# An S5 state-space mixer on one core: the sums for a transposed matrix move from TensorE to GpSimd, and the normed input is made in three parts in three different pairs

## The chip, the cores and the metric

One core of one Trainium2 chip. The metric is the device time of one execution in microseconds (us), and the median of three runs stands for a kernel. The engines are named as in the profile: PE is TensorE, DVE VectorE, ACT ScalarE, POOL GpSimd, and SP is SyncE, whose queue issues most of the DMAs.

## The reference, cut to what matters

The reference is one inference step of a two-layer diffusion backbone for 1,024 noisy tokens and 128 context tokens with 1,024 channels. Layer 0 mixes the tokens with an S5 state-space layer in two directions, layer 1 with a Fourier transform, and a gated convolutional FFN follows each. Only the S5 mixer is touched here:

```python
def s5_direction(u, lam_re, lam_im, log_dt, b_re, b_im, c_re, c_im, h0, reverse):
    dt = jnp.exp(log_dt)[:, None]
    abar = jnp.exp(lam * dt)                      # (64 groups, 64 states), complex
    bbar = ((abar - 1.0) / lam)[..., None] * bmat  # (groups, states, 16 channels)
    bu = jnp.einsum('blgc,gpc->blgp', u, bbar)
    bu = bu.at[:, edge].add(abar * h0)
    _, h = lax.associative_scan(_linear_recurrence, (a, bu), axis=1, reverse=reverse)
    y = jnp.real(jnp.einsum('gcp,blgp->blgc', cmat, h))
    return y, h[:, edge]
# h = rms_norm(x, g_mix) * (1 + sc1) + sh1 is the input u; both directions are summed,
# a diagonal term is added, then GELU and a gated linear layer (GLU)
```

## The kernel before, in words

The schedule is written out by hand (`manual_schedule`): each engine executes its instructions in the order in which the program emits them, and semaphores come from the tiles that instructions share.

The mixer works in frames of 8 tokens. A frame's 8 tokens and a group's 16 channels are one axis of 128, and the recurrence goes from frame to frame, 128 frames for the sample and 16 for the context (146 columns with the edges). The 64 groups go in 8 batches (b = 0 to 7) of 8 groups, and a batch in 4 pairs of groups (pr = 0 to 3). One turn of the loop in `run` is one pair i = 4b + pr. It emits, in this order:

- `vmm(i+1)`: 16 products on PE with the transposed input matrix `PT` (L1503) into one of two PSUM tiles `V`
- `scan(i)` on DVE (L1544), `vin(i+1)` on DVE (L1524 to L1527, a rotation by the tables `sn` and `cs`; L1524 reads `sn`, L1525 reads `cs`), with four small ACT copies behind it, and `vout(i)` on DVE (L1555 to L1557)
- `decay(i+2)` on ACT (L1539), `wmm(i-1)`: 36 products on PE (L1567, L1573) and their eviction `ysb` on ACT (L1579)
- then two lists, `fill` and `late`, with pieces that make the matrices of the batches to come. `vin(i+1)` of pair 3 belongs to the next batch already, and reads that batch's tables.

The pieces, with who executes them:

- `make_u(b)` makes the normed input `hb`: part 0 is one product for the context (t0 = 8), parts 1 and 2 are four products each (L1475, on PE), each part in a PSUM bank of tag "misc" with an ACT eviction (L1479). `load_u(b)` sends `hb` to the tile `u` by 8 DMAs; `load_x(b)` fetches the tile `xb`, of which there is one.
- `make_ca(b)` returns pieces of the output matrix `CA`: five on GpSimd (L1365 to L1370, of which `ca[3:]` are L1369 and L1370), `ends` (four ACT copies, L1374 and L1375) and a pair `bb`. `bb[0]` (`real`) makes the real part of `Bb` (L1383 to L1385, on GpSimd for b > 2), `bb[1]` makes the imaginary part on DVE (L1383 to L1385 again), then L1392 and L1393 on DVE, both of which read the real part too, and an ACT copy (L1394).
- `make_p(b)` returns the products `P` (L1417, three of 128x512 for each half, on GpSimd for b > 1, with one small sum L1412 ahead) and the transposes `tr` (L1425): for each half two calls, each of which fills one "misc" bank and evicts it on ACT (L1428) into `PT`. Half 0 is used by pairs 0 and 1, half 1 by pairs 2 and 3.
- `make_t(b)`: 64 products on PE (L1447) in both "misc" banks, six ACT evictions (L1457 to L1459), two small sums on GpSimd (L1460, L1461) and DMAs that spread the result.
- `tables(b)`: `tb[0]` (L1308, L1309 on DVE), `tb[1]` (L983, L984 on DVE and an ACT op), `tb[2]` (`sn`) and `tb[3]` (`cs`), both on ACT (L1322).

There are two "misc" banks. A piece that takes one of them again waits until its last content has been evicted. In the kernel before the pieces lie so, for a batch b from 1 to 5: pair 0 has the products of half 0, `tb[0]`, `bb[0]`; pair 1 the products of half 1, `ca[:1]`, the transposes of half 0 and `tb[1:]`; pair 2 `bb[1]`, `ca[1:3]`, `make_t` and the transposes of half 1; pair 3 `ca[3:]`, `ends`, all three parts of `make_u` and `load_x`.

Of the kernel before, what the change touches and what calls it, by code (L numbers as in the profile page):

```python
# [13 lines left out]
OP = mybir.AluOpType  # L14
# [950 lines left out]
class Ssm:  # L965
# [431 lines left out]
    def make_p(self, b):  # L1397


        nc, sp, V = self.nc, self.sp, self.nc.vector  # L1400
        gs = slice(8 * b, 8 * b + 8)
        Bb, Bx = self.Bb[b], self.Bx[b]
        PT = self.PT[b] = [sp.tile([128, 2, 4, 128], F32, tag=f"PT{h}", bufs=1, name="PT") for h in range(2)]
        x = [t[:, :, None, :].to_broadcast([128, 8, 8, 16]) for t in (Bb[:, 0, :, 0], Bx[:, 1], Bx[:, 0])]
        qs, Ps = [], {}
        E = nc.gpsimd if b > 1 else V

        def prod(h, i):
            def f():
                if not qs:  # L1410
                    qs.append(self.sg.tile([128, 8, 8], F32, tag="gs", bufs=1, name="gs"))
                    E.tensor_tensor(qs[0], self.G[:, 0, gs], self.G[:, 1, gs], OP.add)  # L1412
                if i == 0:
                    Ps[h] = self.sg.tile([128, 3, 4, 8, 16], F32, tag="P", bufs=2, name="P")
                g = (qs[0], self.G[:, 1, gs], self.G[:, 0, gs])[i]
                hs = slice(4 * h, 4 * h + 4)
                E.tensor_tensor(Ps[h][:, i], g[:, hs, :, None].to_broadcast([128, 4, 8, 16]), x[i][:, hs], OP.mult)  # L1417
            return f

        def tr(ri, half):  # L1420
            def f():
                p = self.bank("misc", 2)
                for i in range(4):
                    for k in (0, 1 + ri):
                        nc.tensor.matmul(p[:, i * 128:(i + 1) * 128],  # L1425
                                         lhsT=Ps[half][:, k, i].rearrange("p a b -> p (a b)"),
                                         rhs=self.ident, start=k == 0, stop=k > 0, is_transpose=True)
                nc.scalar.activation(PT[half][:, ri].rearrange("p a b -> p (a b)"), p, AF.Copy)  # L1428
            return f
        return [[prod(h, i) for i in range(3)] for h in range(2)], [[tr(ri, h) for ri in range(2)] for h in range(2)]  # L1430

    def make_t(self, b):

# [31 lines left out]
            src = bass.AP(tensor=self.kd.tensor, offset=o + (7 - t) * 16, ap=[[240, 16], [32 * 240, 8], [1, 128]])  # L1465
            nc.sync.dma_start(T[16 * t:16 * t + 16], src)

    def make_u(self, b, between=None):

        nc, sp = self.nc, self.sp  # L1470
        x, h = self.xb[b] if b else [t[:, :128] for t in self.xt], self.hb
        for t0, n in ((8, 1), (4, 4), (0, 4)):
            p = self.bank("misc", 2)
            for i in range(n):
                nc.tensor.matmul(p[:, 128 * i:128 * i + 128], lhsT=x[t0 + i], rhs=self.R[:, t0 + i], start=True, stop=True)  # L1475
            if n == 1 and between:
                between()
            o, c = (h[:, t0:t0 + 4, 0:128], 0) if n > 1 else (h[:, :, 130:146], 1)
            nc.scalar.activation(o, p[:, :128 * n].rearrange("p (t k) -> p t k", t=o.shape[1]), AF.Identity,  # L1479
                                 scale=self.a1[:, b, c:c + 1], bias=self.b1[:, b, c:c + 1])  # L1480
            if n == 1:

                nc.scalar.activation(h[:, 7, 128:129], h[:, 0, 130:131], AF.Copy)
                nc.scalar.activation(h[:, 0, 129:130], h[:, 7, 145:146], AF.Copy)
# [108 lines left out]
    def run(self):  # L1593
# [16 lines left out]
        ca, ends, bb = self.make_ca(0)  # L1610
# [6 lines left out]
        pp, tr = self.make_p(0)  # L1617
        tb = self.tables(0)
# [8 lines left out]
        ca1, ends1, bb = self.make_ca(1)  # L1627
# [17 lines left out]
        tb = self.tables(1)  # L1645
# [4 lines left out]
        n = 32  # L1650
        for i in range(n + 1):
            b, pr = divmod(i, 4)
            n1, n2 = b + 1 < 8, b + 2 < 8
            if 1 < i + 1 < n:
                self.vmm(i + 1)
            if i < n:
                self.scan(i)
            if i + 1 < n:
                self.vin(i + 1)
            if i < n:  # L1660
                self.vout(i)
            if i + 2 < n:
                self.decay(i + 2)
            if i:
                self.wmm(i - 1)
            while self.m_ada:
                self.ada_end()
            if i == n:
                self.store_y(b - 1)
                self.n.want(("g", 1), self.nc.vector)  # L1670
                break
            if i == 27:
                self.made.__exit__(None, None, None)
            fill, late = [], []
            if pr == 0:
                if n1 and b:
                    self.load_u(b + 1)
                if b:
                    self.store_y(b - 1)
                if n1:  # L1680
                    pp, tr = self.make_p(b + 1)
                    fill = list(pp[0])
                    if b:
                        tb = self.tables(b + 1)
                        fill += tb[:1]
                if n2 and b:
                    ca, ends, bb = self.make_ca(b + 2)
                    fill.append(lambda: bb[0](self.nc.gpsimd))
                if not b:
                    fill += ca1[2:] + [ends1]  # L1690
                    second = Later(self.nc.vector)
                    self.phases(second, rest)
                    self.phases16(second, rest)
                    late = tr[0] + tb[2:3] + [lambda: self.powers(rest, [second])]
            if pr == 1:
                if n1:
                    fill = list(pp[1])
                    late = tr[0] + tb[1:] if b else tb[3:]
                if not b:
                    ca, ends, bb = self.make_ca(2)  # L1700
                if n2:
                    fill += ca[:1]
                    if b + 3 < 8:
                        self.loads(b + 3)
            if pr == 2:
                if n1:
                    late = [lambda: self.make_t(b + 1)()] + tr[1]
                if n2:
                    if not b:
                        bb[0]()  # L1710
                    bb[1]()
                    fill = ca[1:3]
            if i == 7:
                late = [self.last_frame]
            if pr == 3 and n2:
                fill = ca[3:] + [ends]
                late.append(lambda: self.make_u(b + 2))
                if b + 3 < 8:
                    late.append(lambda: self.load_x(b + 3))
            if i >= 27:  # L1720
                late.append(lambda: self.n.early(i - 27))
            call(fill)
            if i == n - 1:
                self.finals()
            call(late)
# [154 lines left out]
```

## Time and profile before

| | us |
|---|---|
| median of 3 runs (2441.09 to 2443.05) | 2441.32 |
| the profiled execution, whole | 2443.08 |
| its span, first to last instruction | 2441.3 |
| PE busy in the span | 2303.3 (94%) |
| DVE busy | 1487.1 (61%) |
| ACT busy | 870.0 (36%) |
| POOL busy | 679.7 (28%) |

The profiled execution lies 1.8 us above the median, and 1.8 us of its time lie outside the span. The mean of PE is that of the whole kernel: the GLU and the two FFNs after the mixer keep PE busy nearly all the time. The mixer ends near 322 us. In its loop, from 100 to 320 us, PE is busy 14.5 to 18.4 us of each 20, and DVE 13.0 to 19.7.

### The profile page before, as it was taken

Reading aid. Unit: us, or ns where it says so; the run is one execution under the profiler, and the core shown is the slowest. Engines: PE = TensorE matmul, PEld = TensorE weight load, DVE = VectorE, ACT = ScalarE, POOL = GpSimd, SP = SyncE. Lnnn points to the kernel's source line nnn. Section 1 sums busy time; section 2 is a strip of 40 time slices with the busy share of each in tenths; the row PEclk is TensorE's granted clock in tenths of the full one; section 3 lists DMA queues with packets and bytes.
Section 4 is the critical chain, followed back from the end, with each engine's and each line's share of the span. In section 5 each row is a group of like instructions: output and inputs, shape, how many; then the busy total and the mean of one; then the engine's idle time right before and its main releaser. Section 6 shows DMA issues by size and latency. Waiting matters only on the chain.

```text
span 2441.3 us, 35730 instructions
## 1 busy us (share of the span) xinstructions
PE 2303.3 (94%) x14754; PEld 2223.2 (91%) x14754; DVE 1487.1 (61%) x2407; ACT 870.0 (36%) x1320; POOL 679.7 (28%) x462
## 2 busy tenths in 40 slices
PE   3788899999999999999999999999999999999996
PEld 3677788788999999999999999899999999999996
DVE  7877869797635555455544574855554455644456
ACT  5555563225432223222232254442223222232234
POOL 6465303234211122112221253521222112221124
PEclk8899999999999999999999999999999999999998
DMA  6432297671110111111110131111111111111112
GB/s 215 123 83 72 74 300 251 225 241 35 61 44 27 44 44 52 35 35 43 44 52 26 53 105 38 44 52 35 44 44 52 35 35 35 52 52 36 28 42 78
DMA packets 94522, 182.33 MB, mean 75 GB/s; under 512 B 16948, under 2 KB 57204, under 8 KB 93336
## 3 DMA queue, kind: packets, MB, share of 16 engines
q1 hardware_dynamic: 90824, 170.67, 22.2%
q0 software_dynamic: 2096, 6.62, 0.8%
q8 instruction: 117, 1.92, 0.3%
q10 hardware_dynamic: 1440, 2.75, 0.3%
q14 instruction: 45, 0.37, 0.0%
HBM read 163.70 MB, written 11.53 MB: 72 GB/s over the span
## 4 chain that ended last, share of the span: by engine, by line
PE 69%; DVE 16%; issue 6%; POOL 3%; DMA 3%; ACT 2%; SPq 1%; DVEq 0%; ACTq 0%; POOLq 0%
PE acc L199 62%; DVE c L308 3%; DVE dl L602 2%; DVE dh L602 2%; PE f L839 2%; DMA w_ada<-w_ada 1%; DVE X L916 1%; DVE h L222 1%; PE f L749 1%; DVE X L363 1%; DVE X L364 1%; POOL P L1417 1%; PE misc L1447 1%; PE f L199 1%; PE V L1503 1%
## 5 line engine op out<-in xcount | busy, mean ns | idle before, releaser
L199 PE MATMUL acc<-h,uh 128*128 128x384 f32 (+1 forms) x4992 | 1016.0, 338 | 0.5 <-ACT ysb L1579 0.5
L199 PEld LDWEIGHTS acc<-h,uh 128*128 128x128 f32 x4992 | 885.9, 188 | 15.0 <-issue 12.0
L183 POOL TENSOR_TENSOR ul<-raw,uh 128x1024 fp32r<-128x1024 f32 x104 | 271.4, 2609 | 1243.3 <-ACT uh L182 1243.3
L199 PE MATMUL acc<-h,ul 128*128 128x384 f32 (+1 forms) x2496 | 571.7, 337 | 0.0
L308 DVE SCALAR_TENSOR_TENSOR c<-t,cw,c 128x896 f32<-128x896 f32 x704 | 347.2, 562 | 202.4 <-ACT c L305 202.4
L199 PEld LDWEIGHTS acc<-h,ul 128*128 128x128 f32 x2496 | 448.8, 189 | 0.0
L182 ACT ACTIVATE uh<-raw 128x1024 fp32r<-128x1024 f32 x108 | 113.7, 1052 | 548.0 <-PE acc L199 495.4
L300 DVE COPY wb<-acc 128x2 f32<-128x2 f32 x88 | 14.0, 159 | 406.3 <-PE acc L199 406.3
L363 DVE SCALAR_TENSOR_TENSOR X<-acc,MOD,X 128x768 f32<-128x768 f32 x168 | 169.8, 1011 | 118.3 <-PE acc L199 118.3
L199 PE MATMUL acc<-gh,dh 128*128 128x384 f32 x960 | 220.7, 337 | 18.4 <-DVE X L365 18.4
L199 PE MATMUL acc<-gl,dh 128*128 128x384 f32 x960 | 218.5, 335 | 0.0
L199 PE MATMUL acc<-gh,dl 128*128 128x384 f32 x960 | 218.3, 334 | 0.0
L199 PEld LDWEIGHTS acc<-gh,dh 128*128 128x128 f32 x960 | 168.8, 188 | 26.9 <-PE acc L199 23.6
L199 PEld LDWEIGHTS acc<-gh,dl 128*128 128x128 f32 x960 | 171.4, 188 | 0.0
L199 PEld LDWEIGHTS acc<-gl,dh 128*128 128x128 f32 x960 | 171.2, 188 | 0.0
L336 ACT ACTIVATE gh<-c 128x1152 fp32r<-128x1152 f32 x44 | 51.4, 1169 | 329.2 <-DVE c L331 290.9
L303 ACT ACTIVATE t<-t,wb 128x1024 f32<-128x1024 f32 x88 | 101.4, 1153 | 152.2 <-DVE t L301 152.2
L183 POOL TENSOR_TENSOR dl<-raw,dh 128x1024 fp32r<-128x1024 f32 x40 | 99.8, 2515 | 165.1 <-ACT dh L182 165.1
L305 ACT ACTIVATE c<-t,cb,cw 128x1152 f32<-128x1152 f32 x88 | 118.9, 1351 | 2.9
L301 DVE TENSOR_TENSOR t<-acc,R 128x1152 f32<-128x1152 f32 x88 | 118.6, 1348 | 0.0
L326 ACT ACTIVATE c<-c 128x1152 f32<-128x1152 f32 x44 | 51.4, 1167 | 152.4 <-DVE c L308 152.3
L602 DVE SCALAR_TENSOR_TENSOR dl<-w_ada,SC,dl 128x1024 f32<-128x1024 f32 x50 | 88.8, 1815 | 0.0
(327 smaller groups left out, 2600.9 us busy)
## 6 DMA issues: line engine op xcount, KB each, us to landing
raw<-w_up SPq DMA_DIRECT2D x88, 512.0 KB, 3.6
w_ada<-w_ada SPq DMA_DIRECT2D x80, 512.0 KB, 4.8
raw<-w_down SPq DMA_DIRECT2D x44, 512.0 KB, 3.6
w_ada<-w_ada SPq DMA_DIRECT2D x8, 1024.0 KB, 5.0
raw<-w_glu SPq DMA_DIRECT2D x16, 512.0 KB, 4.7
u<-hb SPq DMA_DIRECT2D x64, 73.0 KB, 2.8
y_scratch<-ysb SPq DMA_DIRECT2D x8, 584.0 KB, 3.9
xt<-x SPq DMA_DIRECT2D x9, 512.0 KB, 8.1
```

What stands on the lines that cost most here:

```text
L182: nc.scalar.activation(hi, raw, AF.Copy)
L183: (E or nc.gpsimd).tensor_tensor(lo, raw, hi.bitcast(F32), OP.subtract)
L199: mm(outs[j], lhsT=w, rhs=r[j], start=first and i == 0, stop=last and i == 2)
L301: nc.vector.tensor_tensor(t.rearrange("p (a b) -> p a b", a=3), p[:, :, :384], self.R.rearrange("p (a b) -> p a b", a=3), OP.mult)
L303: nc.scalar.activation(t[:, :NS], t[:, :NS], AF.Identity, bias=wb[:, 0:1])
L305: nc.scalar.activation(c, t, AF.Identity, bias=cb[:, ui:ui + 1], scale=w(1))
L308: nc.vector.scalar_tensor_tensor(o, a, w(i), o, op0=OP.mult, op1=OP.add)
L326: nc.scalar.activation(c, c, AF.Silu)
L336: nc.scalar.activation(gh, c, AF.Copy)
L363: nc.vector.scalar_tensor_tensor(v, p[:, 0:2, :384], s(0), v, op0=OP.mult, op1=OP.add)
L602: nc.vector.scalar_tensor_tensor(o, i, a, o, op0=OP.mult, op1=OP.add)
L839: nc.tensor.matmul(o, lhsT=l, rhs=x, start=kd not in seen, stop=n == last[kd], skip_group_check=True)
```

## The change

The sums that PE made by accumulating two transposes in one bank are made by GpSimd ahead of the transposes for the batches b > 1: four more sums of 128x512 in a batch, and 16 transposes instead of 32. The three parts of `make_u` for a batch are issued in pairs 1 and 3 of one batch and pair 0 of the next. `make_ca`, with its two sums L1356 and L1357, moves to pair 2, and both halves of `bb` to pair 3. The transposes of half 1 move from pair 2 to pair 3, and `tb[3:]` (`cs`) from pair 1 to pair 2.

```diff
+        def sums(h):
+            def f():
+                for i in (1, 2):
+                    E.tensor_tensor(Ps[h][:, i], Ps[h][:, i], Ps[h][:, 0], OP.add)
+            return f
...
-                    for k in (0, 1 + ri):
+                    for k in ((0, 1 + ri) if b < 2 else (1 + ri,)):
...
-                                         rhs=self.ident, start=k == 0, stop=k > 0, is_transpose=True)
+                                         rhs=self.ident, start=k == 0 or b > 1, stop=k > 0, is_transpose=True)
...
-    def make_u(self, b, between=None):
+    def make_u(self, b, between=None, parts=(0, 1, 2)):
...
-        for t0, n in ((8, 1), (4, 4), (0, 4)):
+        for t0, n in [((8, 1), (4, 4), (0, 4))[k] for k in parts]:
...
             if pr == 0:
                 if n1 and b:
+                    self.make_u(b + 1, parts=(2,))
+                    if b + 2 < 8:
+                        self.load_x(b + 2)
                     self.load_u(b + 1)
...
-                if n2 and b:
-                    ca, ends, bb = self.make_ca(b + 2)
-                    fill.append(lambda: bb[0](self.nc.gpsimd))
...
             if pr == 1:
                 if n1:
                     fill = list(pp[1])
-                    late = tr[0] + tb[1:] if b else tb[3:]
-                if not b:
-                    ca, ends, bb = self.make_ca(2)
+                    late = tr[0] + tb[1:3] if b else tb[3:]
                 if n2:
-                    fill += ca[:1]
                     if b + 3 < 8:
                         self.loads(b + 3)
+                    late.append(lambda: self.make_u(b + 2, parts=(0,)))
             if pr == 2:
                 if n1:
-                    late = [lambda: self.make_t(b + 1)()] + tr[1]
+                    late = [lambda: self.make_t(b + 1)()]
+                    if b:
+                        late += tb[3:]
                 if n2:
-                    if not b:
-                        bb[0]()
-                    bb[1]()
-                    fill = ca[1:3]
+                    ca, ends, bb = self.make_ca(b + 2)
+                    fill = ca[:3]
...
-            if pr == 3 and n2:
-                fill = ca[3:] + [ends]
-                late.append(lambda: self.make_u(b + 2))
-                if b + 3 < 8:
-                    late.append(lambda: self.load_x(b + 3))
+            if pr == 3 and n1:
+                late += tr[1]
+                if n2:
+                    bb[0](self.nc.gpsimd if b else self.nc.vector)
+                    bb[1]()
+                    fill = ca[3:] + [ends]
+                    late.append(lambda: self.make_u(b + 2, parts=(1,)))
```

## Rows read from the trace of the kernel before

**Rows 1.** The view by stages: one batch of the mixer, from the scan of its pair 0 to the scan of the next batch's pair 0. The columns are the stretch, its length, the busy time of PE, PE's weight loads, DVE, ACT and POOL with their instructions, the granted clock of PE, the DMA share and GB/s.

```profile
171.42:205.51 34.09, 28.38 (x325) 24.96 (x324) 26.98 (x43) 17.76 (x59) 20.36 (x21) 0.95 0.29 78
```

**Rows 2.** DVE in order of time in this batch, from `tb[0]` in pair 0 to the rotation of the next batch's second pair. The columns are start, duration, engine, line, operation and shape, and in brackets the idle time before it with what ended it.

```profile
179.30 1.36 DVE L1308 COPY w<-W 128x144 f32<-128x144 f32 x1
...
183.33 1.38 DVE L1544 TENSOR_TENSOR_SCAN V<-dec,V 128x592 f32<-128x592 f32 x1
...
188.00 0.45 DVE L1557 SCALAR_TENSOR_TENSOR C<-V,sn 128x292 f32<-128x292 f32 x1
...
195.09 0.28 DVE L1383 TENSOR_TENSOR Bb<-Bm,beta 128x128 f32<-128x128 f32 x1
...
196.41 1.39 DVE L1544 TENSOR_TENSOR_SCAN V<-dec,V 128x592 f32<-128x592 f32 x1
201.74 0.77 DVE L1524 TENSOR_TENSOR B<-V,sn 128x584 f32<-128x584 f32 x1 [3.94 <-PE V L1503]
202.42 0.77 DVE L1525 TENSOR_TENSOR V<-V,cs 128x584 f32<-128x584 f32 x1
...
205.14 0.45 DVE L1557 SCALAR_TENSOR_TENSOR C<-V,sn 128x292 f32<-128x292 f32 x1
...
209.61 0.77 DVE L1524 TENSOR_TENSOR B<-V,sn 128x584 f32<-128x584 f32 x1 [2.72 <-PE V L1503]
```

**Rows 3.** PE in order of time, from `vmm` in pair 2 to `vmm` in pair 0 of the next batch; the same columns.

```profile
188.51 2.22 PE L1503 MATMUL V<-u,PT 128*64 128x146 f32 x16 [3.08 <-DVE C L1557]
190.66 1.33 PE L1567 MATMUL y<-u,T 128*128 128x146 f32 x4
...
194.10 4.33 PE L1447 MATMUL misc<-CA,Bb 64*32 64x128 f32 x64
198.60 1.94 PE L1425 MATMUL misc<-ident,P 128*128 128x128 f32 x16 [0.18 <-issue]
200.47 1.22 PE L1503 MATMUL V<-u,PT 128*64 128x146 f32 x16
201.62 0.77 PE L1567 MATMUL y<-u,T 128*128 128x146 f32 x4
...
204.50 1.38 PE L1475 MATMUL misc<-rstd,xb 128*128 128x128 f32 x10
207.26 1.16 PE L1475 MATMUL misc<-rstd,xb 128*128 128x128 f32 x8 [1.38 <-ACT hb L1479]
208.35 1.22 PE L1503 MATMUL V<-u,PT 128*64 128x146 f32 x16
```

**Rows 4.** ACT in order of time: in pair 1 the eviction of the transposes of half 0 and the table `cs`, in pair 2 the copy of `bb[1]`, the last eviction of `make_t` and the first one of half 1, in pair 3 the first copy of `ends` and the first eviction of `make_u`.

```profile
189.04 1.07 ACT L1428 ACTIVATE PT<-misc 128x512 f32<-128x512 f32 x2
...
192.49 1.82 ACT L1322 ACTIVATE cs<-wa,hpi 128x516 f32<-128x516 f32 x4
...
196.09 0.41 ACT L1394 ACTIVATE Bb<-Bb 128x256 f32<-128x256 f32 x1
...
198.70 0.27 ACT L1459 ACTIVATE kc<-misc 128x112 f32<-128x112 f32 x1
199.70 0.60 ACT L1428 ACTIVATE PT<-misc 128x512 f32<-128x512 f32 x1 [0.73 <-PE misc L1425]
...
206.18 0.24 ACT L1374 ACTIVATE CA<-Cm 128x64 f32<-128x64 f32 x1
...
206.76 0.44 ACT L1479 ACTIVATE hb<-misc,b,a 128x128 f32<-128x128 f32 x1
```

**Rows 5.** POOL in order of time, from `make_t`'s first sum in pair 2 to the products of half 1.

```profile
198.89 0.25 POOL L1460 TENSOR_TENSOR k<-k,DD 128x32 f32<-128x32 f32 x1 [13.26 <-ACT k L1458]
...
199.43 1.93 POOL L1369 TENSOR_TENSOR CA<-Qt,Cx 128x1024 f32<-128x1024 f32 x1
201.44 2.36 POOL L1370 TENSOR_TENSOR CA<-CA,CAt 128x1024 f32<-128x1024 f32 x1
...
204.58 0.32 POOL L1412 TENSOR_TENSOR gs<-Gt 128x64 f32<-128x64 f32 x1
204.98 1.06 POOL L1417 TENSOR_TENSOR P<-gs,Bb 128x512 f32<-128x512 f32 x1
...
208.03 0.40 POOL L1383 TENSOR_TENSOR Bb<-Bm,beta 128x128 f32<-128x128 f32 x1
...
209.28 1.05 POOL L1417 TENSOR_TENSOR P<-gs,Bb 128x512 f32<-128x512 f32 x1
```

**Rows 6.** Ahead of the loop, where DVE and POOL are both busy: two instructions of `bb` for batch 0 on DVE.

```profile
24.95 2.01 DVE L1384 TENSOR_TENSOR Bx<-Bm,beta 128x128 f32<-128x128 f32 x1
26.99 1.90 DVE L1385 TENSOR_TENSOR Bb<-Bb,Bx 128x128 f32<-128x128 f32 x1
```

**Rows 7.** POOL in the same stretch.

```profile
24.75 2.05 POOL L1366 TENSOR_TENSOR CAt<-qs,Cm 128x1024 f32<-128x1024 f32 x1
26.77 1.97 POOL L1367 TENSOR_TENSOR CA<-Qt,Cx 128x1024 f32<-128x1024 f32 x1
```

**Rows 8.** DVE in pair 0 of batch 6, where POOL has nothing to do: `tb[0]` and the scan behind it.

```profile
281.56 0.22 DVE L1308 COPY w<-W 128x144 f32<-128x144 f32 x1
...
282.70 1.38 DVE L1544 TENSOR_TENSOR_SCAN V<-dec,V 128x592 f32<-128x592 f32 x1
```

**Rows 9.** The view by lines, POOL alone, after 300 us: a sum of 128x512 with two whole inputs. The columns are line, engine, operation, tiles, shape and count, then busy us and the mean ns of one, then idle time before with its releaser.

```profile
L170 POOL TENSOR_TENSOR wf<-raw 128x512 f32<-128x512 f32 x7 | 12.0, 1718 | 11.3 <-PE f L749 11.3
```

More of the change, by code (lines that the diff above doesn't have):

```diff
@@ L1423, in f @@
                 for i in range(4):
-                    for k in (0, 1 + ri):
+                    for k in ((0, 1 + ri) if b < 2 else (1 + ri,)):
                         nc.tensor.matmul(p[:, i * 128:(i + 1) * 128],
                                          lhsT=Ps[half][:, k, i].rearrange("p a b -> p (a b)"),
-                                         rhs=self.ident, start=k == 0, stop=k > 0, is_transpose=True)
+                                         rhs=self.ident, start=k == 0 or b > 1, stop=k > 0, is_transpose=True)
                 nc.scalar.activation(PT[half][:, ri].rearrange("p a b -> p (a b)"), p, AF.Copy)
             return f
-        return [[prod(h, i) for i in range(3)] for h in range(2)], [[tr(ri, h) for ri in range(2)] for h in range(2)]
+        return [[prod(h, i) for i in range(3)] + ([sums(h)] if b > 1 else []) for h in range(2)], [[tr(ri, h) for ri in range(2)] for h in range(2)]
     def make_t(self, b):
```

## The prediction

> **What bounds the kernel now.** I read the view by stages first, then each engine in order of time, because the share of busy time hides that the mixer and the rest have different limits. After the mixer PE is nearly always busy with work that the change doesn't touch, and that begins when the mixer ends; so what the mixer gains or loses is taken to reach the end one to one. In the mixer one batch takes 34.09 us [rows 1], and no engine is full: PE works 28.38, DVE 26.98, POOL 20.36, ACT 17.76. The reader is to see that DVE and PE hand the work to each other: `vin` waits for `vmm`, `vmm` for the `vout` before it. On DVE [rows 2] two waits stand out, 3.94 us at the rotation in pair 3 and 2.72 us at the one in pair 0, both for `vmm` on PE. PE's order [rows 3] says why: in pair 2 `make_t` and the transposes of half 1 stand ahead of `vmm`, in pair 3 `make_u`, whose third part waits 1.38 us until ACT has emptied a "misc" bank. DVE loses time to a third thing: `tb[0]` takes from 179.30 to 183.33, 4.03 us [rows 2], where POOL works, and 1.14 us (281.56 to 282.70) where it doesn't [rows 8].
>
> So a batch has three places. I follow each from one end of `vout` to the next thing that DVE waits for.
>
> **Place 1: from `vout` of pair 1 to the rotation of pair 3.** `vout` ends at 188.45 (188.00 + 0.45), L1525 begins at 202.42 [rows 2]. Removed: the transposes of half 1, 1.87 us from 198.60 to 200.47 [rows 3]. Added: part 0 of `make_u`, at the end of pair 1 and so ahead of `vmm` of pair 2 on PE. Ten entries of L1475 take 1.38 and eight 1.16 [rows 3], so its two are 0.2 us; but it is the third piece in a row that takes a "misc" bank, and needs the bank of the first transposes of half 0. ACT begins to empty these at 189.04 and takes 1.07 for two [rows 4], so the bank is free at 189.58 and `vmm` starts at about 189.9 instead of 188.51 [rows 3]: 1.4 us late. `make_t`'s end, M, goes from 198.43 (194.10 + 4.33) to 199.83. Then comes the moved `cs`: it stands behind `make_t`'s evictions on ACT, the last of which ends 0.54 after M (198.70 + 0.27) [rows 4], and takes 1.82 [rows 4], so L1525, which reads `cs`, can't begin before M + 2.4 = 202.2. Without `cs` it could at M + 2.1: a gap of 0.17 [rows 3], `vmm` up to L1524, 1.27 (200.47 to 201.74), and 0.68 to L1525 [rows 2, 3]. Gain: 0.2 us a batch. Bounds: 1.6 if the bank is no hindrance (L1525 at 200.84), 0 if part 0 and `vmm` go slower.
>
> `tb[1]` on DVE now meets POOL's large products, at worst two in a row, 1.93 + 2.36 us [rows 5]. I cost this at nothing: DVE idles 3.94 us in this place [rows 2], and `bb`, 1.32 us (195.09 to 196.41), leaves it. Without that cover it would cost up to 4.3 us a batch.
>
> **Place 2: from `vout` of pair 3 to the rotation of pair 0.** Before: 205.59 (205.14 + 0.45) to 209.61, 4.02 us [rows 2]. Two parts of `make_u` leave, 0.2 and 1.1 us of PE with a bank wait of 1.38 [rows 3], one stays; the transposes of half 1 come, half of 1.94 [rows 3]. But `bb[0]`, `bb[1]` and `ends` now come first, and the order decides.
>
> - POOL: L1460 runs 0.46 after M and L1369 1.00 after it (199.43) [rows 5]. `bb[0]` goes between, 1.25 us (208.03 to 209.28) [rows 5]. So L1369 begins at M + 2.25, L1370 2.01 later, and ends at M + 6.62 [rows 5].
> - DVE: L1525 begins at M + 2.4 and `vout` ends 3.17 later (202.42 to 205.59) [rows 2]: M + 5.6. Call this E. `bb[1]` is next, in the middle of L1370.
> - The rows ahead of the loop show such instructions beside POOL: 2.01 and 1.90 us [rows 6] instead of 0.28 [rows 2], each ending about when one POOL product ended [rows 7]. I take it that DVE and POOL alternate: a wait of 1.0 for L1370, 0.2, the sum L1412 0.4, 0.3, the product 1.05 [rows 5], 0.3. The imaginary part is there at E + 3.3, all of `bb[1]` at E + 3.7, against 1.32 alone [rows 2].
> - ACT: the copy L1394 waits for the imaginary part. Behind it stand `ends` and only then the evictions of the transposes: about 0.4 [rows 4], 0.58 (206.18 to 206.76) [rows 4] and 0.60 [rows 4]. The bank is free at E + 4.9.
> - PE: part 1, third to ask for a bank, waits for that, takes 1.09 (207.26 to 208.35), and `vmm` up to the rotation 1.26 (208.35 to 209.61) [rows 3]. The rotation begins at E + 7.2 and not at 4.02: 3.2 us lost. DVE would have been ready at E + 5.1 (`bb[1]` and a scan of 1.39 [rows 2]).
>
> The clock adds to this. After 3.08 us of idling PE's 16 products took 2.22 us, against 1.22 at 200.47, and the next four 1.33, against 0.77 [rows 3], the lower of the two levels in place of 2.4 GHz; the granted clock of the batch is 0.95 [rows 1]. In the changed order PE idles from M + 5.2 (0.17 + 4.03 from 200.47 to 204.50 + 0.97 [rows 3]) to M + 10.5, longer than that. The same fall costs 1.0 + 0.56, so 4.8 lost in all. I take 4.0, the middle of 3.2 and 4.8, since ACT's instructions overlap by a little. Lower bound: if POOL doesn't hold `bb[1]` up, the imaginary part is there at E + 0.8, the bank at E + 2.4, the rotation at E + 4.8: 0.8 lost.
>
> No row shows whether a short sum or a 512-wide product holds DVE up as the large products of [rows 7] did. The Trainium skill, SBUF — State Buffer, "Who interferes with whom", says that a VectorE instruction with two inputs in SBUF and a GpSimd instruction that reads SBUF exclude each other for the whole instruction, whichever began first. By that all three waits are real and place 2 loses the 4.0; if the large ones alone counted, it would lose 1.4 less a batch, and the sum below would be 2450.
>
> **Place 3: `tb[0]` in pair 0.** The two DVE instructions met two products of 128x1024, now they meet products of 1.05 [rows 5] and the new sums. No row shows such a sum in the mixer: from below 1.05, a product of that size [rows 5], from above 1.72 [rows 9]; I take 1.35. `tb[0]` then waits half of one, 0.5, and one whole, 1.2, beside its own 1.14 [rows 8]: 2.8 instead of 4.03, a gain of 1.2 in batches 2 to 5 (bounds 0 and 2.9). In batch 6, where POOL was free [rows 8], it now meets products and sums: 1.7 lost.
>
> **Costed at nothing.** The 16 transposes saved in pair 1, half of 1.94, end before an idle stretch of 3.08 us on PE [rows 3]. The four sums, 5.4 us a batch, fit on POOL: it idles 13.26 in a batch before L1460 [rows 5]. Part 2 in pair 0 ends while DVE is at `tb[0]`. On SP `load_x` now waits for part 2's products and stands ahead of `load_u`, `store_y` and `loads`; `xb` is wanted a pair later, `u` three pairs later. If `xb` came late, each us would stand on PE ahead of pair 2.
>
> **The sum.** Place 2 for the five passages after batches 1 to 5: 5 x 4.0 = 20.0. Place 1 in batches 1 to 6: -1.2. Place 3: -4.8 + 1.7 = -3.1. Batch 0, where other work fills the turns, I leave out. Together +15.7 on the profiled 2443.08 (span 2441.3 and 1.8 around it), which is 1.8 above the median: 2457 as a median.
>
> **The rivals.**
> - *The bank waits don't happen* (other side). If ACT emptied the banks before PE asks again, place 1 would gain 1.6 six times; in place 2 DVE would set the rotation, at E + 5.1: 1.1 lost five times. With place 3: -9.6 + 5.5 - 3.1 = -7, 2434. It decides at 188.45 in pair 1 and at E in pair 3: the eviction must end by then. For it speaks that ACT is busy for only 17.76 of 34.09 [rows 1]; against it that the eviction at 189.04 begins after 188.45 [rows 4], and that the third part waits now.
> - *DVE isn't held up at `bb`*, since POOL is through when DVE comes: 5 x 0.8 - 1.2 - 3.1, no change, 2441. For it: POOL has spare time. Against: L1370 is tied to M as E is, and ends 1.0 after E.
> - *The sums cost 1.72 and `tb[0]` falls behind two*: 1.72 + 1.72 + 1.14 = 4.6, 0.6 lost four times and 3.5 once, +5.9 instead of -3.1: 2466. For it: two sums stand behind each other at the end of each half. Against: products are as many.
>
> **How the numbers follow.** The forecast has 0.64, the bank rival 0.12, the free `bb` 0.11, the dear sums 0.13. The range takes in the forecast with its bounds and the dear sums, and reaches down to the free `bb`: 2442 to 2468. By 0.2% (4.9 us, about what a measurement of this kernel can tell from no change): slower 0.77, within 0.11, faster 0.12.
>
> **What would show it.** In the changed profile: about 36.5 us a batch; the wait at the rotation in pair 3 down to 2 or 3 us, that in pair 0 up (its releaser still `vmm`); L1475 on PE waiting for ACT's eviction of `PT` in pairs 1 and 3; the five `bb` instructions over 3 us long together; `tb[0]` below 3.5. The prediction is wrong if the evictions come before PE asks, or if `bb` meets no POOL instruction.

## The result and the profile after

The changed kernel takes 2457.05 us (median of 4 runs, 2452.48 to 2458.65); the kernel before, in the same sessions, 2441.4 (4 runs, 2441.09 to 2443.05). The ratio is 1.006 with a 95% interval of 1.0042 to 1.0077: slower, at the predicted 2457. The profiled execution took 2455.93, with a span of 2453.9, so 12.85 more than the profiled one of before.

The diff adds six lines ahead of the mixer's instructions, so every line from L1420 on is six higher here: the rotation L1524 and L1525 is L1530 and L1531, `vmm` L1503 is L1509, `make_u` L1475 is L1481, the transposes L1425 and their eviction L1428 are L1431 and L1434, the scan L1544 is L1550, the end of `vout` L1557 is L1563. L1423 is the new sum.

The view by stages, one batch of the mixer of the changed kernel (from `bb` in pair 3 to `bb` in the next pair 3), with the columns of [rows 1]:

```profile
209.49:246.00 36.51, 28.39 (x306) 24.77 (x306) 29.33 (x43) 17.73 (x59) 25.93 (x25) 0.91 0.34 83
```

The batch was 34.09 [rows 1] and is 36.51, where the prediction said about 36.5. It is the middle of an uneven row: from scan to scan batches 2 to 5 take 37.77, 35.54, 36.50 and 36.94, before 35.05, 34.09, 34.09 and 34.07. PE is busy as long as before although it makes sixteen transposes less; its clock is lower (0.91 against 0.95). POOL works 5.6 us more, DVE 2.35 more on the same 43 instructions.

**Place 2, where the time is lost.** DVE in order of time in the changed kernel, from the end of `vout` in pair 3 to the rotation in pair 0:

```profile
209.12 0.45 DVE L1563 SCALAR_TENSOR_TENSOR C<-V,sn 128x292 f32<-128x292 f32 x1
209.49 1.38 DVE L1383 TENSOR_TENSOR Bb<-Bm,beta 128x128 f32<-128x128 f32 x1
210.79 0.40 DVE L1384 TENSOR_TENSOR Bx<-Bm,beta 128x128 f32<-128x128 f32 x1
211.23 1.09 DVE L1385 TENSOR_TENSOR Bb<-Bb,Bx 128x128 f32<-128x128 f32 x1
...
212.84 1.39 DVE L1550 TENSOR_TENSOR_SCAN V<-dec,V 128x592 f32<-128x592 f32 x1
...
217.91 0.77 DVE L1530 TENSOR_TENSOR B<-V,sn 128x584 f32<-128x584 f32 x1 [3.69 <-PE V L1509]
```

POOL in the same stretch:

```profile
208.36 2.36 POOL L1370 TENSOR_TENSOR CA<-CA,CAt 128x1024 f32<-128x1024 f32 x1
210.68 0.37 POOL L1412 TENSOR_TENSOR gs<-Gt 128x64 f32<-128x64 f32 x1
211.12 1.05 POOL L1417 TENSOR_TENSOR P<-gs,Bb 128x512 f32<-128x512 f32 x1
...
215.02 2.48 POOL L1423 TENSOR_TENSOR P<-P 128x512 f32<-128x512 f32 x2
```

ACT, with the copy of `bb[1]` and the evictions of the transposes:

```profile
212.41 0.42 ACT L1394 ACTIVATE Bb<-Bb 128x256 f32<-128x256 f32 x1 [2.16 <-DVE Bb L1385]
...
213.32 1.06 ACT L1434 ACTIVATE PT<-misc 128x512 f32<-128x512 f32 x2
```

And PE:

```profile
208.05 1.10 PE L1431 MATMUL misc<-ident,P 128*128 128x128 f32 x8
213.95 1.94 PE L1481 MATMUL misc<-rstd,xb 128*128 128x128 f32 x8 [4.79 <-ACT PT L1434]
215.82 2.04 PE L1509 MATMUL V<-u,PT 128*64 128x146 f32 x16
```

Read the four in one chain. The three stretched instructions of `bb` end at 210.87, 211.19 and 212.32; POOL's three end at 210.72, 211.05 and 212.17. Each time DVE is through 0.14 to 0.15 after POOL: it waits its turn, and three short instructions, the first of which takes 0.28 alone [rows 2], take 1.38, 0.40 and 1.09. ACT's copy waits 2.16 for them, the evictions of the transposes stand behind the copy and `ends`, and part 1 of `make_u` on PE waits 4.79 for a bank that these evictions free. Then PE comes back near the lower of its clock levels (granted 0.56 from 213.95 to 217.86): part 1 takes 1.94 and not 1.16 [rows 3], `vmm` 2.04 and not 1.22. DVE waits 3.69 at the rotation, 8.34 after `vout`'s end, where it was 4.02.

**Place 3, where some comes back.** DVE at `tb[0]` of the next batch:

```profile
221.68 0.22 DVE L1308 COPY w<-W 128x144 f32<-128x144 f32 x1
221.82 2.16 DVE L1309 TENSOR_TENSOR w<-W,ph 128x896 f32<-128x896 f32 x1
223.91 1.38 DVE L1550 TENSOR_TENSOR_SCAN V<-dec,V 128x592 f32<-128x592 f32 x1
```

That is 2.23 (223.91 less 221.68) in place of 4.03.

**Place 1, two lengths.** PE at the end of pair 1 in two batches of the changed kernel:

```profile
195.11 0.49 PE L1481 MATMUL misc<-rstd,xb 128*128 128x128 f32 x2 [3.06 <-DMA u<-hb]
195.53 1.22 PE L1509 MATMUL V<-u,PT 128*64 128x146 f32 x16
...
230.26 0.49 PE L1481 MATMUL misc<-rstd,xb 128*128 128x128 f32 x2 [3.32 <-ACT PT L1434]
230.67 1.75 PE L1509 MATMUL V<-u,PT 128*64 128x146 f32 x16
```

The view by stages of what follows these waits, and of what follows a wait of 4.80 in place 2 of the next passage; PE's granted clock is the third number from the end:

```profile
195.11:197.37 2.26, 2.26 (x22) 1.79 (x22) 2.23 (x3) 0.44 (x1) 0.65 (x1) 1.00 0.93 288
230.26:233.63 3.37, 3.37 (x22) 2.57 (x23) 3.37 (x2) 1.30 (x2) 1.52 (x1) 0.64 0.81 261
250.45:255.52 5.07, 5.07 (x28) 4.26 (x29) 1.07 (x3) 1.21 (x2) 5.07 (x6) 0.54 0.02 3
```

In both batches part 0 waits for its bank: it starts 1.22 and 1.23 after `vout`'s end, as soon as ACT has emptied the first bank of the transposes (in the first batch the profile names a DMA that had also just ended). But after 3.06 us of waiting the clock stayed at 1.00, after 3.32 it was 0.64. With it go 1.4 us of place 1. The places of all batches, each worked out as a difference of two times of DVE in the two traces (place 2 is the passage to the next batch):

```
batch   place 1           place 2           place 3
        before  after     before  after     before  after
0       18.80   17.28     5.86    7.62      the same
1       14.18   12.62     5.69    8.84      1.59    2.30
2       13.91   13.87     4.03    8.65      3.37    2.33
3       13.97   12.49     4.02    8.34      4.03    2.30
4       13.98   13.87     4.03    8.64      4.02    2.23
5       13.98   13.90     4.03    8.64      4.00    2.31
6       12.72   10.70     1.32    1.32      1.14    2.03
```

Place 2 loses 23.1, place 1 gains 6.8, place 3 gains 4.7: +11.6. The first of these scans began 0.8 late and pair 1 of batch 1 lost 0.3. That makes 12.7 of the 12.82 by which the mixer's last scan is later (319.17 and 331.99), and the span is 12.6 longer: here what the mixer loses reaches the end. For small differences between other kernels that can't be taken for granted: from the mixer's last scan to the end the fourteen profiled executions take between 2118.2 and 2124.2 us (2122.1 before, 2121.9 in the change), though no edit touches that part.

### The profile page after: what moved, and what is told of

The parts are those of the page before. It is cut to its first block, busy times and chain, and to the rows that moved or that the text cites. A ratio compares the mean times of both kernels' runs of the same rounds, so it can differ in the third digit from the quotient of the medians.

```text
span 2453.9 us, 35559 instructions
## 1 busy us (share of the span) xinstructions
PE 2301.6 (94%) x14658; PEld 2217.4 (90%) x14658; DVE 1502.4 (61%) x2407; ACT 869.1 (35%) x1320; POOL 719.5 (29%) x486
## 3 DMA queue, kind: packets, MB, share of 16 engines
q1 hardware_dynamic: 90824, 170.67, 22.5%
## 4 chain that ended last, share of the span: by engine, by line
PE 71%; DVE 17%; issue 4%; DMA 3%; ACT 3%; SPq 1%; POOL 1%; DVEq 0%; ACTq 0%; POOLq 0%
PE acc L199 62%; DVE c L308 3%; PE f L839 2%; DVE dh L602 1%; DMA w_ada<-w_ada 1%; DVE dl L602 1%; PE misc L1453 1%; DVE X L916 1%; PE V L1509 1%; PE y L1579 1%; PE f L749 1%; DVE h L222 1%; DVE X L363 1%; DMA X<-xT 1%; DVE X L364 1%
## 5 line engine op out<-in xcount | busy, mean ns | idle before, releaser
L183 POOL TENSOR_TENSOR ul<-raw,uh 128x1024 fp32r<-128x1024 f32 x104 | 280.3, 2695 | 1242.6 <-ACT uh L182 1237.1
```

The source lines that it names most:

```text
L183: (E or nc.gpsimd).tensor_tensor(lo, raw, hi.bitcast(F32), OP.subtract)
```

## The experiments

Diffs of `a_...` are against the changed kernel, of `b_...` against the kernel before. Each time is the median of 4 to 11 runs; ratios are to the kernel before, measured in the same session. What an edit takes off the change is counted from `after_again`, whose session is that of `a_order`, `a_ca2` and `a_u0`; counted from the first 2457.05 each figure is 2.6 larger.

**The changed kernel once more** (`after_again`).

> The changed kernel once more, as the base for the runs beside it: 2457 us as before, within 2452 to 2459.

2454.43 us, ratio 1.0057 (1.0045 to 1.007). Its profiled execution repeats the table above batch by batch to within 0.05 us: which batch has the long place 1 is no accident of one trace.

**Part 1 ahead of `bb`** (`a_order`): in pair 3 the transposes of half 1 and part 1 are issued first, `bb` and `ends` after them.

```
+                    late.append(lambda: self.make_u(b + 2, parts=(1,)))
+                    call(late)
+                    late = []
                     bb[0](self.nc.gpsimd if b else self.nc.vector)
                     bb[1]()
                     fill = ca[3:] + [ends]
-                    late.append(lambda: self.make_u(b + 2, parts=(1,)))
```

> The changed kernel with one order altered: in pair 3 the transposes of half 1 with their evictions and part 1 of make_u are emitted ahead of bb and ends, not behind them. GpSimd and VectorE meet at bb as before. Theory of the prediction (the price of place 2 is the bank that ACT empties only behind bb): the bank is free about 1.2 us after vout of pair 3 instead of 4.9, PE no longer sets the rotation, which then begins when VectorE is through bb, 3.35 us, and a scan, 1.4 us: 4.8 us after vout instead of 8.4. That is 3.6 us in five passages, 18 us: 2439. Rival (the price is the waiting of VectorE at bb alone, the bank wait only fills the same time): nothing gained, 2457.

2441.95 us, ratio 1.0006 (0.9997 to 1.0015): the slowdown is gone. DVE and PE of this kernel in place 2:

```profile
204.99 1.38 DVE L1383 TENSOR_TENSOR Bb<-Bm,beta 128x128 f32<-128x128 f32 x1
...
208.34 1.39 DVE L1550 TENSOR_TENSOR_SCAN V<-dec,V 128x592 f32<-128x592 f32 x1
209.64 0.75 DVE L1530 TENSOR_TENSOR B<-V,sn 128x584 f32<-128x584 f32 x1
```

```profile
206.29 1.16 PE L1481 MATMUL misc<-rstd,xb 128*128 128x128 f32 x8 [1.64 <-ACT PT L1434]
207.38 1.22 PE L1509 MATMUL V<-u,PT 128*64 128x146 f32 x16
```

`bb` is as slow as in the change, 3.35 from 204.99 to the scan, but PE no longer waits for it: it waits 1.64 and not 4.8, keeps its clock, and the rotation follows the scan at once, 4.57 after `vout`. So most of the loss is not `bb` by itself but that PE's bank stands behind it. In the two profiled executions place 2 falls by 21.0 in all, more than the 18 expected; place 1 takes 7.7 of it back (15.1 to 15.3 in batches 3 to 5, where part 0 still waits 3.62 and `vmm` behind it takes 2.22), place 3 another 2.0. By the medians 12.5 are left.

**The large products out of `bb`'s way** (`a_ca2`): all of `ca` in pair 2, so that POOL has done L1369 and L1370 when DVE comes to `bb[1]`.

```
-                    fill = ca[:3]
+                    fill = ca
...
-                    fill = ca[3:] + [ends]
+                    fill = [ends]
```

> The changed kernel with one move: L1369 and L1370 are issued by GpSimd in pair 2 with the rest of make_ca, so that nothing large stands between bb[0] and the products of the next batch. The order on ACT stays. Theory: GpSimd has done bb[0], the small sum and the first product before VectorE comes to bb, the five instructions take 1.3 us instead of 3.35, the imaginary part comes 2.1 us sooner, and with it the whole chain over ACT to the bank: 2 to 3.5 us in five passages, 2440 to 2447. Rival (VectorE is held up elsewhere by as much, the two large products meeting tb[1] in pair 1 instead): 2455 or more.

2449.19 us, ratio 1.0038 (1.0025 to 1.005): between the two. DVE, then PE, of this kernel in place 2:

```profile
211.65 0.28 DVE L1383 TENSOR_TENSOR Bb<-Bm,beta 128x128 f32<-128x128 f32 x1
...
212.97 1.39 DVE L1550 TENSOR_TENSOR_SCAN V<-dec,V 128x592 f32<-128x592 f32 x1
...
217.89 0.77 DVE L1530 TENSOR_TENSOR B<-V,sn 128x584 f32<-128x584 f32 x1 [3.53 <-PE V L1509]
```

```profile
214.09 2.07 PE L1481 MATMUL misc<-rstd,xb 128*128 128x128 f32 x8 [2.78 <-ACT PT L1434]
```

`bb` is back to 1.32 (212.97 less 211.65), which alone shows that POOL had held it up, and place 2 falls by 1.5 to 2.5 in the passages after batches 1 to 5, to between 6.1 and 7.3. But the bank wait (2.78) and the low clock (2.07) stay, and the products now meet `tb[1]`, which takes 5 us in batches 1, 2 and 5. Place 1 gives back 8.4 in all: 3.3 in these three batches, 3.8 in batch 0, and 1.4 in batch 3, where `tb[1]` stayed at 3.7 but `vmm` now takes 1.85 and not 1.22. The prediction had costed this meeting at nothing in the changed order; it is nothing only while `tb[1]` stays near 3.5.

**Part 0 in pair 0** (`a_u0`): together with part 2.

```
-                    self.make_u(b + 1, parts=(2,))
+                    self.make_u(b + 1, parts=(0, 2))
...
-                    late.append(lambda: self.make_u(b + 2, parts=(0,)))
```

> The changed kernel with part 0 of make_u issued in pair 0 of the next batch ahead of part 2, not at the end of pair 1. Theory: PE no longer waits 3.3 us for a bank ahead of vmm in pair 2, which starts 1.4 us sooner, with make_t behind it: 1.4 us in six batches, 2449. Rival (tb[1], 3.7 us long beside GpSimd's large products, sets the rotation of pair 3 by itself, or cs does): nothing, 2457.

2446.11 us, ratio 1.0023 (1.0015 to 1.0032): 8.3 less than `after_again`, as much as expected. PE and DVE of this kernel in place 1:

```profile
191.63 1.22 PE L1509 MATMUL V<-u,PT 128*64 128x146 f32 x16 [1.94 <-DVE C L1563]
```

```profile
203.33 0.78 DVE L1531 TENSOR_TENSOR V<-V,cs 128x584 f32<-128x584 f32 x1 [1.13 <-ACT cs L1322]
```

`vmm` follows `vout` at once and at the full clock, place 1 is 11.8 in batches 2 to 4, and now `cs` sets the rotation. Part 0 had cost more than its bank wait: place 1 is 1.9 to 2.1 shorter in batches 2, 4 and 5, where with the wait the fall of the clock goes too, and 0.7 to 1.0 in batches 1 and 3, where there was none.

**Both** (`a_both`): the two edits together.

> The changed kernel with both repairs: in pair 3 the transposes and part 1 of make_u are emitted ahead of bb and ends, and part 0 is issued in pair 0 of the next batch. Theory: the two bank waits stand at different places of the batch and their prices add, -12.5 and -8.3 as each alone: 2434 to 2436. Rival (one wait hides the other, or VectorE becomes the bound with bb held up and tb[1] at 4 us): 2440 or more.

2433.36 us, ratio 0.9971 (0.9959 to 0.9984). The single edits took off 12.5 and 8.3, together 21.1: additive. With part 0's wait gone and part 1's down to 2.4 to 3.5, the change is faster than the kernel before.

**Without the sums** (`a_nosums`): the changed order, the products summed by the transposes as before (32 transposes a batch).

```
-                    for k in ((0, 1 + ri) if b < 2 else (1 + ri,)):
+                    for k in (0, 1 + ri):
...
-        return [[prod(h, i) for i in range(3)] + ([sums(h)] if b > 1 else []) for h in range(2)], ...
+        return [[prod(h, i) for i in range(3)] for h in range(2)], ...
```

> The changed kernel without the sums on GpSimd: PE accumulates two transposes again, 32 in a batch, everything else as changed. Theory: the sums cost and save next to nothing here, since the transposes end ahead of PE's waits for the bank (3.3 us in pair 1, 4.8 us in pair 3) and GpSimd idles 9.3 us a batch: 2457, within 3. Rival (the sums on GpSimd are what makes the kernel slow, by holding VectorE up): 2449 or less.

2453.84 us, ratio 1.0049 (1.0036 to 1.0061): the intervals of this and of the change overlap. The sums did not make the change slow; leaving them out brings nothing that can be told from the scatter.

**The sums alone** (`b_sums`): the same lines the other way about, put into the kernel before.

> The kernel before with the sums on GpSimd alone, nothing moved. Theory: in pair 2 the transposes of half 1 stand on the path ahead of vmm there, and half as many save 0.85 us in six batches, 5 us; tb[0] in pair 0 meets products of 1.05 us instead of products of 1.93 us, as GpSimd is 5 us further back, and takes about 2.6 us instead of 4.03: 1.4 us in five batches, 7 us. Together 2429. Rival (GpSimd falls behind and holds up make_t or the transposes): 2441 or more.

2438.72 us (2435.35 to 2447.37), ratio 0.9995 (0.9984 to 1.0005): no difference that can be measured, where 2429 was expected. `tb[0]` of this kernel:

```profile
210.52 0.31 DVE L1308 COPY w<-W 128x144 f32<-128x144 f32 x1
210.75 1.95 DVE L1309 TENSOR_TENSOR w<-W,ph 128x896 f32<-128x896 f32 x1
```

In the profiled execution batches 3 to 5 take 31.84 in place of 34.09, most of it here (2.10 and not 4.03), but batch 2 gains nothing and batch 6 loses 1.8. The profiled last scan is 5.6 earlier, the median only 3.0. The eleven times scatter more than those of any other kernel here: four lie between 2435.35 and 2435.64, the profiled one among them, two at 2438.6 and 2438.7, five between 2442.42 and 2447.37. What the slower executions do otherwise was not seen and stays open.

**The split alone** (`b_split`): the kernel before with `make_u` in three pairs as in the change; `bb` and the transposes of half 1 stay in pair 2.

```
             if pr == 0:
                 if n1 and b:
+                    self.make_u(b + 1, parts=(2,))
+                    if b + 2 < 8:
+                        self.load_x(b + 2)
...
             if pr == 1:
...
+                    late.append(lambda: self.make_u(b + 2, parts=(0,)))
...
             if pr == 3 and n2:
                 fill = ca[3:] + [ends]
-                late.append(lambda: self.make_u(b + 2))
-                if b + 3 < 8:
-                    late.append(lambda: self.load_x(b + 3))
+                late.append(lambda: self.make_u(b + 2, parts=(1,)))
```

> The kernel before with make_u in three pairs alone (part 0 in pair 1, part 1 in pair 3, part 2 and load_x in pair 0 of the next batch), nothing else moved. Theory: in pair 3 only part 1 is left, its bank is free, vmm follows vout at once and the wait of 2.7 us at the rotation of pair 0 goes, five to six times: -15. In pair 1 part 0 waits for the bank and vmm of pair 2 is 1.4 us late in six batches: +8. Together 2434. Rival (the split itself makes the changed kernel slow): 2445 or more.

2428.49 us, ratio 0.9954 (0.994 to 0.9967): faster. Place 2 is 1.3 and not 4.0; DVE of this kernel there:

```profile
200.32 0.45 DVE L1557 SCALAR_TENSOR_TENSOR C<-V,sn 128x292 f32<-128x292 f32 x1
200.69 1.39 DVE L1544 TENSOR_TENSOR_SCAN V<-dec,V 128x592 f32<-128x592 f32 x1
202.09 0.77 DVE L1524 TENSOR_TENSOR B<-V,sn 128x584 f32<-128x584 f32 x1
```

Neither the split nor the sums (`a_nosums`) make the loss, so it is the rest of the change, the moves of `bb` with `make_ca`, of the transposes of half 1 and of `cs`, that turns it into one. They were not all tried one by one; `b_pair0` below has the transposes in pair 3 and is fast. PE of this kernel at the end of pair 1:

```profile
214.77 0.49 PE L1475 MATMUL misc<-rstd,xb 128*128 128x128 f32 x2 [2.77 <-ACT PT L1428]
215.19 1.22 PE L1503 MATMUL V<-u,PT 128*64 128x146 f32 x16
```

Part 0's bank wait is here too: place 1 takes 15.5, 1.5 more than before.

**The split without that wait** (`b_split02`): as `b_split`, with part 0 in pair 0 too. Against `b_split`:

```
-                    self.make_u(b + 1, parts=(2,))
+                    self.make_u(b + 1, parts=(0, 2))
...
-                    late.append(lambda: self.make_u(b + 2, parts=(0,)))
```

> The kernel before with make_u in two pairs, part 1 in pair 3, parts 0 and 2 with load_x in pair 0, and no sums on GpSimd: the run with part 0 in pair 1 gave 2428.5. There vmm of pair 2 started 1.7 us late, but at full clock (1.22 us), while in the kernel before it starts at once and takes 2.22, with 0.56 more lost behind it. Theory: without part 0 PE idles through to vmm, the clock falls, and the 1.6 us come back: 2427 to 2430. Rival (the bank wait was a loss by itself): 1.4 us in five batches, 2421.

2418.37 us, ratio 0.9906 (0.9892 to 0.9919). The theory that the bank wait taken away would be paid for by the clock is wrong, and the rival holds. The view by stages, one batch of this kernel:

```profile
195.84:225.48 29.64, 26.73 (x324) 23.76 (x322) 26.85 (x42) 17.48 (x59) 20.47 (x21) 1.00 0.45 103
```

The granted clock is 1.00 over the whole batch, where it was 0.95 [rows 1]. Place 1 is 13.76, so part 0 in pair 1 had cost 1.7 a batch. Against this kernel the last scan of `a_both` is 12.2 later (310.10 and 297.93): its place 2 takes 4.6 to 6.5 a passage and not 1.3, 19 us in all, and its place 1 wins 11 back. So `bb` in pair 3 costs DVE time of its own: 4.57 even in the passage after batch 3, where the rotation follows the scan at once.

**The sums on top** (`b_best`): the edits of `b_sums` and of `b_split02` together, in the kernel before.

> The kernel before with the sums on GpSimd and with make_u in two pairs: part 1 in pair 3, parts 0 and 2 with load_x in pair 0 of the next batch; bb, make_ca, cs and the transposes stay where they were. Theory: the gains of the two parts add and no bank wait comes in: -12 for the sums, -15 for the wait at the rotation of pair 0: 2414 to 2418. Rival (what one wait gives back the next takes): 2430 or more.

2423.1 us, ratio 0.9928 (0.9915 to 0.994): slower than without them. PE of this kernel, behind `make_t`, in two batches in a row:

```profile
188.59 1.06 PE L1431 MATMUL misc<-ident,P 128*128 128x128 f32 x8 [2.38 <-issue]
...
217.60 1.94 PE L1431 MATMUL misc<-ident,P 128*128 128x128 f32 x8 [2.39 <-issue]
219.47 1.89 PE L1509 MATMUL V<-u,PT 128*64 128x146 f32 x16
```

In the second of them eight transposes take as long as sixteen did in [rows 3] (the granted clock is 0.56 from 217.60 to 221.30), after a wait as long as that of the first; place 1 is 15.29 there and 13.73 in the first. Batch 6 takes 29.54, where it takes 27.27 without the sums. The gain of `b_sums`' steady batches doesn't add to that of the split. But of the 8.0 by which the profiled span is longer than that of `b_split02` only 2.6 lie ahead of the mixer's last scan (300.50 and 297.93), and this profiled execution was the slowest of five: what makes the other part was not found.

**All of `make_u` in pair 0** (`b_pair0`): with the sums, and the transposes of half 1 in pair 3, `bb` left in pair 2.

```
             if pr == 0:
                 if n1 and b:
+                    self.make_u(b + 1)
+                    if b + 2 < 8:
+                        self.load_x(b + 2)
...
             if pr == 2:
                 if n1:
-                    late = [lambda: self.make_t(b + 1)()] + tr[1]
+                    late = [lambda: self.make_t(b + 1)()]
...
-                late.append(lambda: self.make_u(b + 2))
-                if b + 3 < 8:
-                    late.append(lambda: self.load_x(b + 3))
+            if pr == 3 and n1:
+                late += tr[1]
```

> The kernel before with the sums on GpSimd, all of make_u in pair 0 ahead of load_u, load_x behind it, and the transposes of half 1 in pair 3; bb, make_ca and cs as before. Nothing waits for a bank behind bb then, and each pair has room for its PE work: 2.6 us and a bank wait in pair 0 (where VectorE has tb[0]), 1.1 in pair 1, make_t alone in pair 2, 1.1 in pair 3. Theory: the waits of VectorE at the rotations of pairs 3 and 0 are under 1 us each, a batch takes about 28.5 us, and the time is 2412 to 2417, less than with the two pairs (2423). Rival (the bank wait among the three parts makes vmm of pair 1 late by as much): 2423 or more.

2415.82 us, ratio 0.9896 (0.9883 to 0.991), the fastest kernel here. Its stages:

```profile
191.76:220.76 29.00, 25.03 (x306) 22.01 (x306) 28.54 (x42) 17.47 (x59) 26.64 (x25) 1.00 0.38 98
```

DVE works 28.54 of 29.00: after the waits for PE are gone, DVE itself is the bound, and part of its time is waiting for POOL inside its instructions.

**The same without the sums** (`b_pair0_nosums`): the edits of `b_pair0` less those of `b_sums`, so 32 transposes a batch again.

> The kernel before with the three pairs of make_u put into pair 0 of the batch, behind the scan's first tile, and the half-1 transposes tr[1] into pair 3; the products stay as before: 32 transposes, no sums on GpSimd. It differs from b_pair0 (2415.8) by the sums alone. Theory one: where no bank wait stands behind the transposes any more, the sums only lengthen GpSimd's work beside VectorE and the four of about 1.25 us cost more than the 16 transposes did, as between b_split02 (2418.4, without) and b_best (2423.1, with): 2409 to 2413. Rival: the transposes come dearer in pair 3, where they stand ahead of the next batch's first matmuls, and the kernel takes 2416 to 2421.

2417.19 us, ratio 0.9906 (0.989 to 0.9923): not to be told from `b_pair0`. My theory, that the sums cost, is wrong in this order; the rival's number came in, but its reason is not shown, for the profiled batches 3 to 5 take 29.13 against 29.00. What differs is where DVE meets POOL; of this kernel:

```profile
207.02 2.15 DVE L983 TENSOR_SCALAR wa<-w 128x896 f32<-128x896 f32 x1
209.20 3.12 DVE L984 TENSOR_TENSOR w<-w,wa 128x896 f32<-128x896 f32 x1
```

`tb[1]` takes 5.2 here and 3.0 with the sums, `tb[0]` 1.4 here and 3.0 with them. What the sums on POOL cost, with the transposes that they save, depends on the order they stand in: -1 to -3 us (`b_sums`, by the ratio and by the medians), +1 to +3 (in the change), +5 (`b_best`, against `b_split02`), -1 (here), of which only the +5 is beyond the scatter.

## Why the prediction was right, step by step

**Place 2** was the step that decided, and it holds link by link: `bb` stretched in turns with POOL (3.3 us, 3.7 predicted), the copy and `ends` in front of the evictions, the bank wait, the clock. It measured 8.3 to 8.8 in the passages after batches 1 to 5 against the forecast's 8.0, and lost 21.3 there against 20.0. Inside it two sizes were off against each other: part 1 starts 4.4 after `vout`, half a us earlier than worked out, and the clock costs 1.6 to 1.9 (0.8 to 0.9 on part 1, which the prediction left at full speed, 0.8 to 1.0 on `vmm`) where the middle value had left room for 0.8. The 0.56 that it counted beside `vmm`'s 1.0 was not on this path: those products stand behind `vmm`, and the rotation begins when `vmm` is done. `a_order` and `a_ca2` show the two links apart: with the bank's eviction ahead of it a slow `bb` costs 0.5 a passage (4.57 against 4.03); with a fast `bb` the wait still costs 2.1 to 2.6 in batches 2 to 5. The short sum of 0.37 and the product of 1.05 held DVE up as the large sum did, which no row of before could show. The Trainium skill, SBUF — State Buffer, "Who interferes with whom", by whose rule all three waits at `bb` were real, agrees with the trace: the ends lie 0.14 to 0.15 us apart.

**Place 1** was mis-sized. The bank wait came (part 0 starts 1.2 us after `vout`'s end, and `vmm` follows 0.4 later, not 0.2), `cs` came last by 0.33 us at the rotation as foreseen, and where the clock fell the gain is 0.04 to 0.11, predicted 0.2:

```profile
241.80 0.77 DVE L1530 TENSOR_TENSOR B<-V,sn 128x584 f32<-128x584 f32 x1 [2.71 <-PE V L1509]
242.90 0.77 DVE L1531 TENSOR_TENSOR V<-V,cs 128x584 f32<-128x584 f32 x1 [0.33 <-ACT cs L1322]
```

(These are DVE's rows in pair 3 of the changed kernel.) But the sum took `vmm` in pair 2 at the low level of [rows 3] in every batch. In batch 1, where part 0 waits only 0.53, and in batch 3 PE kept the high one, and the gain was 1.5 to 1.6, near the upper bound of 1.6 that I had tied to the bank. In batch 6 there is no part 0, which the term "batches 1 to 6" overlooked: 2.0. Together -5.3 and not -1.2. `tb[1]` did double, from 1.66 to 3.5 to 3.7, and was hidden, as said.

**Place 3.** A sum took 1.24 (2.48 for two), 1.35 was assumed; `tb[0]` took 2.2 to 2.3 and not 2.8. Batches 2 to 5 gained 6.3, not 4.8; batch 6 lost 0.9, not 1.7, as only one instruction waited there; batch 1, left out, lost 0.7.

**Left out.** Batch 0: +1.8 in its passage, -1.5 in its place 1, and 0.8 before it; 0.3 in pair 1 of batch 1.

So by the two profiled executions the change costs 12.85 and the sum said 15.7: place 1 is 4.1 too high, place 3 1.6, place 2 1.3 too low, and the left-out parts add 1.4. By the medians it is 15.65, in the second session 13.7 (2454.43 less 2440.7). That the forecast met the first median to the microsecond is luck: its errors have opposite signs. What held is the mechanism of place 2, which decides the sign.

**The rivals.** That the bank waits don't happen: they do, 3.1 to 3.4 us in pair 1 of batches 2 to 5 and 4.8 to 5.0 in pair 3. That `bb` isn't held up: it is. The dear sums: 1.24 and not 1.72. And of what the prediction costed at nothing, the 16 transposes saved and the four sums that replace them bring together nothing that could be measured, neither in the changed order (`a_nosums`) nor in that of before (`b_sums`). No run has the one without the other.

## What to carry to other kernels

An engine that takes a shared PSUM bank waits for whatever stands ahead of that bank's eviction in the evicting engine's order: before a piece of work is moved, list who evicts the bank that it will get, and what this engine does first. Splitting work into smaller pieces over more stages gains most where each piece finds its bank free: `make_u` in pieces gave 13 us with one piece that waits for its bank (`b_split`) and 22.5 with that piece put elsewhere (`b_split02`), and the two edits of the change that only moved a piece past a busy eviction were worth 12 and 8 us. And a short instruction of VectorE can pay for what GpSimd runs beside it: here three of five in a row each waited for one GpSimd instruction, and the row took 3.35 us and not 1.32. Such a row is best put where GpSimd is idle, or where no other engine waits for its result.

## What the runs showed of the hardware

- Two waits of PE of nearly one length, 3.06 and 3.32 us, were followed by a granted clock of 1.00 and of 0.64, the same way in both profiled executions of the changed kernel. The length of the wait alone doesn't decide it: in `a_both` part 1 waited 2.46 in two passages and took 1.16 and 2.08, with granted clocks of 1.00 (201.72 to 203.90) and 0.58 (265.94 to 269.60). What does was not tried.

```profile
201.72 1.16 PE L1481 MATMUL misc<-rstd,xb 128*128 128x128 f32 x8 [2.46 <-ACT PT L1434]
...
265.94 2.08 PE L1481 MATMUL misc<-rstd,xb 128*128 128x128 f32 x8 [2.46 <-ACT PT L1434]
```

- DVE's waits beside POOL are not those of two-input instructions alone: L983 with one tile as input takes 2.15 us in `b_pair0_nosums` and 0.61 in the changed kernel at 228.95; L1308, a copy, takes 1.11 there at 258.50 and 0.22 at 221.68.
- A sum of two whole 128x512 inputs takes POOL 1.24 us, a product of that size with one broadcast input 1.05; seen by its shape alone, [rows 9] had put it at 1.72.
